# The two-chunk scan of a hybrid trunk, taken as one chunk, with the logs of scan and forgetting summed together

## The chip, the cores and the metric

The kernel runs on one core of one Trainium2 chip, on TensorE (PE), VectorE (DVE), ScalarE (ACT), GpSimd (POOL) and the DMA queues, which SyncE (SP) and ACT feed. The metric is device time in microseconds, the median of several runs; lower is better.

## The reference, cut to what matters

A trunk of two residual layers over 256 tokens of width 1024. Each layer projects the normalised stream by one wide matrix and feeds three causal mixers: a state-space scan (16 heads of 64, 4 groups that share keys `b` and queries `c` of 128 states, chunks of 128 tokens), sliding-window attention, and forgetting attention (16 heads). Their outputs are projected, gated, merged and added to the stream.

```python
def ssd_chunked_scan(xh, dt, a, bm, cm):
    ...
    x_dt = x * dtc[..., None]
    ...
    a_cum = jnp.cumsum(a_dt, axis=-1)
    seg = a_cum[..., :, None] - a_cum[..., None, :]
    decay = jnp.where(causal, jnp.exp(jnp.where(causal, seg, 0.0)), 0.0)
    cb = jnp.einsum('bclgn,bcsgn->bgcls', cc, bc)
    y_diag = jnp.einsum('bgrcls,bcsgrp->bclgrp', cb[:, :, None] * decay, x_dt)
    decay_states = jnp.exp(a_cum[..., -1:] - a_cum)
    states = jnp.einsum('bcsgn,bgrcs,bcsgrp->bcgrpn', bc, decay_states, x_dt)
    ...
    prev = jnp.moveaxis(prev, 0, 1)
    y_off = jnp.einsum('bclgn,bcgrpn,bgrcl->bclgrp', cc, prev, jnp.exp(a_cum))
    return (y_diag + y_off).reshape(b, s, g, r, p)

def forgetting_attention_branch(q, k, v, f_logit, z, f_bias):
    log_f = jax.nn.log_sigmoid((f_logit + f_bias).astype(jnp.float32))
    cum = jnp.transpose(jnp.cumsum(log_f, axis=1), (0, 2, 1))
    ...
        sc = sc + cum[:, :, start:end, None] - cum[:, :, None, :end]
```

Here `a_dt` is `dt` times `a`, the decay logs, summed within a chunk, and `prev` the states, carried from chunk to chunk. With 256 tokens there are two chunks, so one state passes from the first to the second. Of the cumulative logs only differences between two tokens enter the result.

## The kernel before, in words

**Dense work.** Nearly all of the time goes to dense products of the stream with the weights. Each weight tile arrives by a DMA of SP (tile `raw`), is rounded by ACT to a high part (`hi`, L265) and DVE subtracts to get the low part (`lo`, L266); a product then takes three passes (stream high with `hi` and `lo`, stream low with `hi`). There are six buffers each for `raw`, `hi` and `lo`. A dense unit has 24 matmuls, of 256 columns (one block of 128 output channels for all tokens) or of 512 (128 tokens); its sum is held in one of three PSUM buffers `mm`. Five more, `mx`, serve all else.

**Order.** PE runs in an order that the program writes out by hand: the dense units one after the other, and between them, or in the middle of a unit, small pieces of the mixers. A piece is a stretch of a Python generator; it comes due at a time of the program's own clock, which adds a cost for each matmul (L91 to L101), plus a delay that the generator yields (`D_CUM` 12, `D_SSD` 8, `D_SSD2` 3, L25 to L29), and `pump` (L130) puts in what is due. The orders of DVE, ACT and POOL come from a scheduler. Every engine works through its own queue in order; DMAs issued by ACT stand in ACT's queue.

**Decay logs**, once per layer (`decay_logits`, L700 to L753). From a dense product come `dt`, the scan's logs `da` and the forgetting logs `lf`, each two chunks of 128 tokens by 16 heads. `tri` is the matrix of ones up to the diagonal. One pair of products sums `da` with tokens on the partitions (`acum`, L741); a second pair sums it with heads on the partitions (L746); three more do so for `lf`, where the second chunk adds the first through `ones` (L748 to L750). ACT copies both into `cum` and stores them to DRAM (`cumd`, L753), from where they are read back spread over all 128 partitions: for the scan at L785, for forgetting attention as `bias` at L932. The sliding-window attention's pieces (scores on 64-row tiles, softmax, transposes of the weights, second product on 64-wide tiles) follow in PE order, then the scan groups, then forgetting attention.

**A scan group** (`ssd_group`, L780 to L842), four per layer, one at a time, three pieces on PE:

- *Transposes* (L790): four of the inputs, which DVE multiplies by `dt` into `xdt` (L791), and one of the keys, `bt`, copied by ACT (L796). DVE and ACT then make, from the logs spread over the partitions (`bcg`, 128 x 4 heads x 256 tokens): the state's weights `ds` and `xds` (L798 to L801), a decay matrix for each chunk (`decs`, four subtractions with the mask `negtri` at L808, the exponential at L810), and `cx`, the second chunk's queries times the decay since its start (L814, L815).
- *Middle piece*, 8 units of the clock later: the state (`bt` with `xds`, copied by ACT at L821) and for each chunk the product of keys and queries, by which DVE multiplies the decay matrix (L826).
- *Output piece*, 3 units later: for each chunk and each pair of heads the products with `xdt`, and for the second chunk with the state (L838); DVE adds each to the skipped input (L839).

The tiles `bcg` have two buffers (tag L4), `decs` and `cx` share seven (L2).

## Time and profile before

| | |
|---|---|
| median of 3 runs | 844.76 us (847.14, 844.76, 844.22) |
| the profiled execution | 844.62 us |
| its span in the trace | 842.9 us |
| granted PE clock | 0.998 of full speed |
| PE busy | 829.5 us, 98% of the span, 5932 instructions |
| weight loads (PEld) | 758.9 us, 90% |
| DVE, ACT, POOL busy | 641.9, 509.2, 125.8 us |
| DMA | 158.41 MB, 188 GB/s in the mean |

Rows of the trace read: start in us, duration in us, engine, line, operation, output tile <- input tiles, the tile shape on PE (rows*columns), output shape, and "xN" for N instructions recorded as one row from the first start to the last end. A fp32 matmul is recorded as two instructions. The rounded passes of the dense units are one each. Ends of matmuls are modelled, so the distance between starts says more than the duration. A row of a group of instructions gives, behind the count, the busy time in us and the mean of one in ns, then the idle time of the engine just before them and what ended it. Line numbers are those of the kernel before.

### The profile page before, as it was taken

The page shows a single profiled execution, that of the slowest core. Times are in us where ns is not written, and L with a number is a line of the kernel's source. Part 1 is how long each engine was busy: PE and PEld are TensorE (multiplying, and loading weights), DVE is VectorE, ACT ScalarE, POOL GpSimd, SP SyncE. Part 2 cuts the span into 40 slices and gives each one's busy share as a digit, 9 for nine tenths or more (in the row PEclk, how much of TensorE's full clock was granted, in tenths as well). Part 3 has the DMA queues.
Part 4 walks back from the last instruction along what each step waited for, and adds up shares of the span by engine and source line. Part 5 has one row for each costly group of instructions (what it writes and reads, how often), then busy time and mean ns, then how long its engine had stood idle before and what let it go on. Part 6 is the DMA issues. An engine that isn't in the chain of part 4 may idle for free.

```text
span 842.9 us, 15995 instructions
## 1 busy us (share of the span) xinstructions
PE 829.5 (98%) x5932; PEld 758.9 (90%) x5932; DVE 641.9 (76%) x1387; ACT 509.2 (60%) x1012; POOL 125.8 (15%) x166
## 2 busy tenths in 40 slices
PE   7999999999999999999999999999999999999996
PEld 7989898999999998888989998899899999988896
DVE  5778897997776679656688879989878667785665
ACT  6466678665666667435555667775557667654442
POOL 7411300000131010210014112000003110121000
PEclk9999999999999999999999999999999999999999
DMA  8576655676465545648677475565855564566632
GB/s 303 162 231 205 198 171 163 201 210 188 144 201 175 172 164 189 213 151 288 206 233 219 149 204 174 152 212 162 250 176 159 167 179 153 158 237 213 212 101 74
DMA packets 126637, 158.41 MB, mean 188 GB/s; under 512 B 12784, under 2 KB 88224, under 8 KB 126560
## 3 DMA queue, kind: packets, MB, share of 16 engines
q1 hardware_dynamic: 109456, 140.79, 53.2%
q10 hardware_dynamic: 17056, 16.49, 6.3%
q8 instruction: 46, 0.75, 0.4%
q14 instruction: 31, 0.25, 0.1%
q0 software_dynamic: 48, 0.13, 0.0%
HBM read 155.22 MB, written 2.16 MB: 187 GB/s over the span
## 4 chain that ended last, share of the span: by engine, by line
PE 88%; DMA 5%; DVE 2%; issue 2%; ACT 1%; POOL 0%; ACTq 0%; SPq 0%; POOLq 0%; DVEq 0%
PE mm L97 75%; PE mx L97 9%; PE mx L101 3%; DMA raw<-in_w_in_dram 3%; DMA raw<-in_w_proj_dram 1%; DVE lo L266 1%; DMA L<-in_x_dram 1%; DVE L L1068 0%; DVE L L1091 0%; ACT hi L260 0%; ACT hi L265 0%; ACTq L260 0%; POOL sm L227 0%; ACT L L216 0%; DVE L L266 0%
## 5 line engine op out<-in xcount | busy, mean ns | idle before, releaser
L266 DVE TENSOR_TENSOR lo<-raw,hi 128x1024 fp32r<-128x1024 f32 x252 | 307.8, 1234 | 93.4 <-ACT hi L265 84.7
L97 PE MATMUL mm<-hi,L 128*128 128x512 f32 (+1 forms) x1344 | 372.8, 363 | 1.9 <-ACT hi L1225 1.4
L97 PE MATMUL mm<-L,hi 128*128 128x256 f32 x1792 | 317.8, 278 | 0.9 <-DVE L L474 0.9
L265 ACT ACTIVATE hi<-raw 128x1024 fp32r<-128x1024 f32 x252 | 262.9, 1055 | 87.1 <-PE mm L97 59.5
L97 PEld LDWEIGHTS mm<-L,hi 128*128 128x128 f32 x1792 | 277.6, 192 | 7.9 <-issue 3.5
L97 PEld LDWEIGHTS mm<-hi,L 128*128 128x128 f32 x1344 | 241.1, 189 | 32.3 <-issue 2.4
L97 PE MATMUL mm<-L,lo 128*128 128x256 f32 x896 | 246.4, 275 | 0.0
L97 PE MATMUL mm<-lo,L 128*128 128x512 f32 (+1 forms) x672 | 241.3, 360 | 1.4 <-POOL lo L1226 1.4
L97 PEld LDWEIGHTS mm<-L,lo 128*128 128x128 f32 x896 | 171.9, 192 | 0.1
L97 PEld LDWEIGHTS mm<-lo,L 128*128 128x128 f32 x672 | 126.9, 189 | 16.4 <-POOL lo L1226 1.9
L939 POOL TENSOR_SCALAR_AFFINE_SELECT bias<-bias 128x128 f32<-128x128 f32 x64 | 38.6, 635 | 269.4 <-DMA bias<-cumd 237.7
L770 DVE SCALAR_TENSOR_TENSOR L<-L,vec,L 128x255 f32<-128x255 f32 (+2 forms) x96 | 47.5, 495 | 3.6 <-ACT L L767 2.2
L97 PE MATMUL mx<-L,L 128*64 128x128 f32 (+1 forms) x384 | 34.4, 314 | 0.0
L963 ACT ACTIVATE L<-L 128x512 f32<-128x512 f32 x24 | 15.1, 630 | 30.1 <-DVE L L962 30.1
L562 ACT ACTIVATE pp<-pp,nm 128x128 f32<-128x128 f32 x64 | 28.2, 443 | 6.9 <-DVE nm L556 6.9
L97 PEld LDWEIGHTS mx<-L,L 128*64 128x64 f32 x384 | 23.0, 136 | 9.4 <-issue 2.0
L637 ACT ACTIVATE pp<-pp,nm 128x128 f32<-128x128 f32 x64 | 25.1, 393 | 10.3 <-DVE nm L630 9.0
L854 ACT ACTIVATE L<-mm 128x256 f32<-128x256 f32 x48 | 18.2, 379 | 19.5 <-PE mm L97 19.4
L662 POOL TENSOR_SCALAR_AFFINE_SELECT L<-L 128x256 f32<-128x256 f32 x16 | 10.2, 639 | 114.5 <-ACT L L660 114.5
L773 ACT ACTIVATE L<-L 128x256 f32<-128x256 f32 x32 | 13.3, 417 | 21.6 <-DVE L L770 20.4
L630 DVE CUSTOM_DVE_ANT_0 pp<-mx,wmask,nsink 128x128 f32<-128x128 f32 x64 | 24.0, 413 | 2.0 <-PE mx L97 2.0
L1008 POOL TENSOR_TENSOR L<-L,L 128x512 f32<-128x512 f32 x8 | 15.9, 1995 | 57.9 <-DVE L L1007 32.1
(184 smaller groups left out, 795.6 us busy)
## 6 DMA issues: line engine op xcount, KB each, us to landing
raw<-in_w_in_dram SPq DMA_DIRECT2D x200, 512.0 KB, 4.5
raw<-in_w_proj_dram SPq DMA_DIRECT2D x48, 512.0 KB, 5.3
raw<-in_w_out_dram SPq DMA_DIRECT2D x16, 512.0 KB, 5.0
L<-cumd ACTq DMA_DIRECT2D x8, 512.0 KB, 3.9
bias<-cumd ACTq DMA_DIRECT2D x16, 256.0 KB, 3.6
L<-in_gate_bias_dram ACTq DMA_DIRECT2D x12, 256.0 KB, 3.8
L<-in_x_dram SPq DMA_DIRECT2D x2, 512.0 KB, 4.9
nwb<-in_norm_w_dram SPq DMA_DIRECT2D x1, 512.0 KB, 5.3
```

What stands on the lines that cost most here:

```text
L97: nc.tensor.matmul(o, a, b, **kw)
L101: nc.tensor.transpose(o, a, i)
L265: keep(act)(hi, src, AF.Copy)
L266: keep(tt)(lo, src, hi.bitcast(F32), op=ALU.subtract)
L562: act(pp[:, i, sl], pp[:, i, sl], AF.Exp, scale=-1.0, bias=nm[:, e:e + 1], accum_out=sums[:, e:e + 1])
L630: nc.vector.tensor_tensor_reduce(out=pp[:, i, sl], in0=score(p, i, b), in1=m, scale=-0.125, scalar=ns[:, i:i + 1], op0=ALU.add, op1=ALU.mi ...
L637: act(pp[:, i, sl], pp[:, i, sl], AF.Exp, scale=-1.0, bias=nm[:, e:e + 1], accum_out=sums[:, e:e + 1])
L770: stt(a[:, s:S], x_[:, 0:S - s], y.vec[:, 16 * j + u:16 * j + u + 1], a[:, s:S], op0=ALU.mult, op1=ALU.add)
L854: act(halves(th), p, AF.Tanh, scale=0.5)
L939: nc.gpsimd.affine_select(out=bias[:, i, dst], in_=bias[:, i, src], compare_op=ALU.is_ge, fill=NEG, base=0, pattern=[[-1, P]], channel_mul ...
L963: act(g, g, AF.Tanh, scale=0.5)
L1008: gtt(m, m, g, op=ALU.add)
```

## The change

**Logs.** They are measured from the middle of the sequence: the second chunk sums from its start (`tri`), the first backwards from its end (`behind`, which is `tri` less one, so that token t gets minus the sum of the tokens after it). No chunk needs the other's total, and `da` and `lf` (times −16 here, where −8 and 2 were used apart) lie in one tile `dl`, so one pair of products, 32 rows high, gives both. The three products for `lf` go, and one of the two copies.

**Scan.** No state is made. The first chunk's keys meet all 256 queries, and the second chunk's keys the second half. So the decay matrices are `dec` (first chunk's keys, 256 queries), made in place in the tile into which the logs are loaded, and `own` (second chunk's, 128 queries). The transposed keys, `ds`, `xds`, `cx`, the state and their copies and products go. The middle piece has two products into one PSUM tile, 256 and 128 columns wide; the output piece has for each pair of heads one PSUM tile of 256 tokens, with one evacuation.

```diff
@@ in the set-up (pools: "st=2" leaves BUFS)
-    negtri = T("negtri", [P, P])
+    negtri = T("negtri", [P, 2 * P])
...
+    behind = T("behind", [P, P])
+    nc.gpsimd.tensor_scalar(behind, tri, -1.0, None, op0=ALU.add)
+    upto = (behind, tri)
-        lf = T("lf", [P, 2, 16])
+        dl = T("dl", [P, 2, 32])
+        da, lf = dl[:, :, 0:16], dl[:, :, 16:32]
         w = T("uw", [P, 2, 32])
         ts(w[:, :, 0:16], u[:, :, 0:16], 0.0, 0.5, op0=ALU.max, op1=ALU.mult)
         tt(y.dt, w[:, :, 0:16], q3[:, :, 0:16], op=ALU.add)
         ts(y.dt, y.dt, 2.0, None, op0=ALU.mult)
         ts(w[:, :, 16:32], u[:, :, 16:32], 0.0, 0.5, op0=ALU.min, op1=ALU.mult)
         tt(lf, w[:, :, 16:32], q3[:, :, 16:32], op=ALU.subtract)
-        ts(lf, lf, 2.0, None, op0=ALU.mult)
-        da = T("da", [P, 2, 16])
+        ts(lf, lf, -16.0, None, op0=ALU.mult)
         tt(da, y.dt, bc(y.nega, 1, 2), op=ALU.mult)
         yield D_CUM
 
         pa = pmx()
         for c in range(2):
-            mm(pa[:, 16 * c:16 * c + 16], tri, da[:, c, :], start=True, stop=True)
+            mm(pa[:, 16 * c:16 * c + 16], upto[c], da[:, c, :], start=True, stop=True)
         y.acum = T("acum", [P, 2, 16])
         act(y.acum, pa[:, 0:32].rearrange("p (t c) -> p t c", t=2), AF.Copy)
-        cum = T("L2", [16, 2, S])
+        cum = T("L1", [32, S])
         pr = pmx()
         for c in range(2):
-            mm(pr[0:16, c * P:(c + 1) * P], da[:, c, :], tri, start=True, stop=True)
-        act(cum[:, 0, :], pr[0:16, 0:S], AF.Copy)
-        pf = pmx()
-        mm(pf[0:16, 0:P], lf[:, 0, :], tri, start=True, stop=True)
-        mm(pf[0:16, P:S], lf[:, 0, :], ones, start=True, stop=False)
-        mm(pf[0:16, P:S], lf[:, 1, :], tri, start=False, stop=True)
-        act(cum[:, 1, :], pf[0:16, 0:S], AF.Copy, scale=-8.0)
-        y.cumd = dr.tile([16, 2, S], F32, name=f"cumd{y.l}", tag=f"cumd{y.l}")
+            mm(pr[0:32, c * P:(c + 1) * P], dl[:, c, :], upto[c], start=True, stop=True)
+        act(cum, pr[0:32, 0:S], AF.Copy)
+        y.cumd = dr.tile([32, S], F32, name=f"cumd{y.l}", tag=f"cumd{y.l}")
         nc.scalar.dma_start(y.cumd, cum)
 
 
...
         yield lambda: not any(m[2] == 1 for m in waiting)
         yield "ssd"
         xdt = T("L2", [P, 2, 256])
-        bcg = T("L4", [P, 4, S])
-        nc.scalar.dma_start(bcg, y.cumd[4 * g:4 * g + 4, 0, :].partition_broadcast(P))
+        dec = T("L4", [P, 4, S])
+        nc.scalar.dma_start(dec, y.cumd[4 * g:4 * g + 4, :].partition_broadcast(P))
         hs = slice(4 * g, 4 * g + 4)
         for t in range(2):
             p = pmx()
...
                 transpose(p[:, j * P:(j + 1) * P], y.xs[:, 2 * g + j, t * P:(t + 1) * P], ident)
             tt(xdt[:, t, :].rearrange("p (h d) -> p h d", h=4),
                p[:, 0:256].rearrange("p (h d) -> p h d", h=4), bc(y.dt[:, t, hs], 2, 64), op=ALU.mult)
+        own = T("L2", [P, 4, P])
+        for h in range(4):
+            stt(own[:, h, :], dec[:, h, P:S], y.acum[:, 1, 4 * g + h:4 * g + h + 1], negtri[:, 0:P], op0=ALU.subtract, op1=ALU.add)
+        act(own, own, AF.Exp)
+        for h in range(4):
+            stt(dec[:, h, :], dec[:, h, :], y.acum[:, 0, 4 * g + h:4 * g + h + 1], negtri,
+                op0=ALU.subtract, op1=ALU.add)
+        act(dec, dec, AF.Exp)
+        yield D_SSD
+
         p = pmx()
-        transpose(p[:, 0:P], y.bcT[:, g, 0:P], ident)
-        bt = T("bt", [P, P])
-        act(bt, p[:, 0:P], AF.Copy)
-        ds = T("ds", [P, 4], bufs=2)
-        tt(ds, bcg[:, :, P - 1], y.acum[:, 0, hs], op=ALU.subtract)
-        act(ds, ds, AF.Exp)
-        xds = T("L1", [P, 256])
-        tt(xds.rearrange("p (h d) -> p h d", h=4), xdt[:, 0, :].rearrange("p (h d) -> p h d", h=4),
-           bc(ds, 2, 64), op=ALU.mult)
-        decs = []
-        for c in range(2):
-            tk = slice(c * P, (c + 1) * P)
-            dec = T("L2", [P, 4, P])
-            for h in range(4):
-                stt(dec[:, h, :], bcg[:, h, tk], y.acum[:, c, 4 * g + h:4 * g + h + 1], negtri,
-                    op0=ALU.subtract, op1=ALU.add)
-            act(dec, dec, AF.Exp)
-            decs.append(dec)
-
-        cx = T("L2", [P, 4, P])
-        act(cx, bcg[:, :, P:S], AF.Exp)
-        tt(cx, cx, bc(y.bcT[:, 4 + g, P:S], 1, 4), op=ALU.mult)
-        yield D_SSD
-
-        p = pmx()
-        mm(p[:, 0:256], bt, xds, start=True, stop=True)
-        st = T("st", [P, 256])
-        act(st, p[:, 0:256], AF.Copy)
-        for c in range(2):
-            tk = slice(c * P, (c + 1) * P)
-            p = pmx()
-            mm(p[:, 0:P], y.bcT[:, g, tk], y.bcT[:, 4 + g, tk], start=True, stop=True)
-            tt(decs[c], decs[c], bc(p[:, 0:P], 1, 4), op=ALU.mult)
+        mm(p[:, 0:S], y.bcT[:, g, 0:P], y.bcT[:, 4 + g, :], start=True, stop=True)
+        mm(p[:, S:S + P], y.bcT[:, g, P:S], y.bcT[:, 4 + g, P:S], start=True, stop=True)
+        tt(dec, dec, bc(p[:, 0:S], 1, 4), op=ALU.mult)
+        tt(own, own, bc(p[:, S:S + P], 1, 4), op=ALU.mult)
         yield D_SSD2
-        for c in range(2):
-            tk = slice(c * P, (c + 1) * P)
-            for j in range(2):
-                u = 2 * g + j
-                py = pmx()
-                for s in range(c + 1):
-                    for i in range(2):
-                        h = 2 * j + i
-                        hc = slice(64 * h, 64 * h + 64)
-                        a, b = (xdt[:, c, hc], decs[c][:, h, :]) if s == 0 else (st[:, hc], cx[:, h, :])
-                        mm(py[64 * i:64 * i + 64, 0:P], a, b, start=(s == 0), stop=(s == c))
-                stt(y.xs[:, u, tk], y.xs[:, u, tk], y.dsk[:, u:u + 1], py[:, 0:P],
-                    op0=ALU.mult, op1=ALU.add)
+        for j in range(2):
+            u = 2 * g + j
+            py = pmx()
+            for s in range(2):
+                for i in range(2):
+                    h = 2 * j + i
+                    mm(py[64 * i:64 * i + 64, s * P:S], xdt[:, s, 64 * h:64 * h + 64],
+                       (dec, own)[s][:, h, :], start=(s == 0), stop=(s == 1))
+            stt(y.xs[:, u, :], y.xs[:, u, :], y.dsk[:, u:u + 1], py[:, 0:S], op0=ALU.mult, op1=ALU.add)
         yield D_EVAC
         tokens["ssd"] += 1
 
...
         for p in range(2):
             bias = T("bias", [P, 2, 3 * P])
             nc.scalar.dma_start(bias[:, :, P:3 * P],
-                                y.cumd[2 * (j + p):2 * (j + p) + 2, 1, :].partition_broadcast(P))
+                                y.cumd[16 + 2 * (j + p):18 + 2 * (j + p), :].partition_broadcast(P))
             bs.append(bias)
         yield D_BDMA
         for bias in bs:
```

The first place is the piece of the decay logs. PE before, with `mm_1005` and `mm_1050` the dense units around it, `mx_1033` the sums by tokens, `mx_1039` and `mx_1043` the two by heads:

```order
L97 MATMUL mm_1005<-L_24_151,hi_907 128x256
L97 MATMUL mx_1033<-da_838,tri_76 128x16 x2
L97 MATMUL mx_1039<-tri_76,da_838 16x128 x2
L97 MATMUL mx_1043<-tri_76,lf_830 16x128
L97 MATMUL mx_1043<-ones_86,lf_830 16x128
L97 MATMUL mx_1043<-tri_76,lf_830 16x128
L97 MATMUL mm_1050<-L_23_150,hi_889 128x256
L97 MATMUL mm_1050<-L_23_150,lo_890 128x256
L97 MATMUL mm_1050<-L_24_151,hi_889 128x256
```

PE of the changed kernel at the same place (`mx_1034` by tokens, `mx_1040` by heads; `L_51_267` and `qt_454` are keys and queries of the sliding-window attention):

```order
L97 MATMUL mm_1006<-L_25_153,hi_908 128x256
L97 MATMUL mx_1034<-dl_832,behind_98 128x16
L97 MATMUL mx_1034<-dl_832,tri_76 128x16
L97 MATMUL mx_1040<-behind_98,dl_832 32x128
L97 MATMUL mx_1040<-tri_76,dl_832 32x128
L97 MATMUL mx_1050<-L_51_267,qt_454 128x128
L97 MATMUL mx_1051<-L_51_267,qt_454 128x128
L97 MATMUL mx_1050<-L_51_267,qt_454 128x256
L97 MATMUL mx_1051<-L_51_267,qt_454 128x256
```

The three products into `mx_1043` are gone, and the attention's scores, which before came after a further dense unit, follow directly. From there to the end of the first scan groups the mixers' pieces stand about one 256-column unit earlier among the dense units.

The second place is the middle and output pieces of scan group 0 on PE. Before (`mm_2142`, `mm_2210` and `mm_2256` are dense units; the middle piece is `mx_2189` to `mx_2196`):

```order
L97 MATMUL mm_2142<-L_24_151,hi_1971 128x256
L97 MATMUL mx_2189<-L_406_2008,bt_2003 128x256
L97 MATMUL mx_2193<-L_239_1165 128x128
L97 MATMUL mx_2196<-L_239_1165 128x128
L97 MATMUL mm_2210<-hi_2073,L_442_2199 128x512
```

and, one 512-column unit further on:

```order
L97 MATMUL mm_2210<-lo_2174,L_442_2199 128x512
L97 MATMUL mx_2236<-L_407_2010,L_399_1990 64x128 x2
L97 MATMUL mx_2240<-L_407_2010,L_399_1990 64x128 x2
L97 MATMUL mx_2244<-L_408_2016,L_399_1990 64x128 x2
L97 MATMUL mx_2244<-L_409_2022,st_2191 64x128 x2
L97 MATMUL mx_2250<-L_408_2016,L_399_1990 64x128 x2
L97 MATMUL mx_2250<-L_409_2022,st_2191 64x128 x2
L97 MATMUL mm_2256<-hi_2073,L_442_2199 128x512
```

In the changed kernel the middle piece is

```order
L97 MATMUL mm_2090<-L_25_153,hi_1999 128x256
L97 MATMUL mx_2125<-L_239_1171 128x256
L97 MATMUL mx_2125<-L_239_1171 128x128
L97 MATMUL mm_2130<-L_24_152,hi_1987 128x256
L97 MATMUL mm_2130<-L_24_152,lo_1988 128x256
L97 MATMUL mm_2130<-L_25_153,hi_1987 128x256
```

and the output piece

```order
L97 MATMUL mm_2188<-lo_2075,L_432_2177 128x512
L97 MATMUL mx_2201<-L_392_1960,L_391_1959 64x256 x2
L97 MATMUL mx_2201<-L_395_1970,L_391_1959 64x128 x2
L97 MATMUL mx_2207<-L_392_1960,L_391_1959 64x256 x2
L97 MATMUL mx_2207<-L_395_1970,L_391_1959 64x128 x2
L97 MATMUL mm_2188<-hi_2143,L_432_2177 128x512
```

The middle piece has two products in place of three, and the output piece four lines in place of six, now in the middle of a 512-column unit (`mm_2188`) and not behind one. DVE at the same place in the changed kernel, from the splits of the weights (L269 of the changed kernel) to the first multiply by keys and queries (L804); L768 and L772 are the convolution, `mx_2125` the middle piece:

```order
L269 TENSOR_TENSOR lo_2075<-raw_1872,hi_2074 128x1024
L768 SCALAR_TENSOR_TENSOR L_404_2033<-L_405_2034,vec_660,L_404_2033 128x255
L269 TENSOR_TENSOR L_433_2178<-L_153_712,L_432_2177 128x2x256
L768 SCALAR_TENSOR_TENSOR L_404_2033<-L_405_2034,vec_660,L_404_2033 128x254
L269 TENSOR_TENSOR lo_2144<-raw_1935,hi_2143 128x1024
L768 SCALAR_TENSOR_TENSOR L_404_2033<-L_405_2034,vec_660,L_404_2033 128x253
L269 TENSOR_TENSOR lo_2162<-raw_1947,hi_2161 128x1024
L772 SCALAR_TENSOR_TENSOR L_364_1826<-L_406_2040,L_404_2033 128x256
L768 SCALAR_TENSOR_TENSOR L_414_2080<-L_415_2081,vec_660,L_414_2080 128x255
L269 TENSOR_TENSOR L_433_2178<-L_153_712,L_432_2177 128x2x256
L768 SCALAR_TENSOR_TENSOR L_414_2080<-L_415_2081,vec_660,L_414_2080 128x254
L804 TENSOR_TENSOR L_392_1960<-L_392_1960,mx_2125 128x1024
```

The multiply is 1024 columns wide, and stands behind three splits in this piece, with one more and the subtractions of the group ahead of these rows.

The third place is ACT, where the logs of scan group 2 are fetched. Before (with what each waits for; `L_515_2562` is group 2's `bcg`):

```order
L265 ACTIVATE hi_2155<-raw_1939 128x1024 [waits DMAHW4_49,PE_49]
L265 ACTIVATE hi_2173<-raw_1951 128x1024 [waits DMAHW5_49,PE_49]
L785 DMA L_515_2562<-cumd_1048 128x4x256 [waits Activation_49]
L773 ACTIVATE L_413_2057<-L_411_2050 128x256 [waits DVE_49]
L766 ACTIVATE L_422_2098<-mm_2060 128x256
L767 ACTIVATE L_421_2097<-mm_2060,vec_658 128x256
L265 ACTIVATE hi_2263<-raw_1963 128x1024 [waits DMAHW6_49,PE_49]
```

and in the changed kernel (`L_492_2493` is group 2's `dec`):

```order
L764 ACTIVATE L_419_2116<-mm_2090 128x256
L765 ACTIVATE L_418_2115<-mm_2090,vec_660 128x256
L268 ACTIVATE hi_2245<-raw_2003 128x1024 [waits DMAHW7_49,PE_49]
L783 DMA L_492_2493<-cumd_1044 128x1024 [waits PE_49]
L771 ACTIVATE L_420_2122<-L_418_2115 128x256 [waits DVE_49,Activation_49]
L764 ACTIVATE L_430_2168<-mm_2130 128x256
L765 ACTIVATE L_429_2167<-mm_2130,vec_660 128x256
L268 ACTIVATE hi_2279<-raw_2060 128x1024 [waits DMAHW0_49,PE_49]
```

The DMA of the changed kernel waits for PE, whose last reading of group 0's `dec` frees the buffer. Before, its buffer was freed by ACT's own exponential, and DVE's subtractions ahead of that.

More of the change, by code (lines that the diff above doesn't have):

```diff
@@ L59, in hybrid_trunk @@
     BUFS = dict(raw=N_RAW, hi=N_SPLIT, lo=N_SPLIT, L8=8, L4=2, L2=7, L1=14, pp=2, qt=4,
-                bias=2, st=2, sm=6)
+                bias=2, sm=6)
     count = [0]
@@ L170, in hybrid_trunk @@
                             pattern=[[1, P]], channel_multiplier=-1)
-    negtri = T("negtri", [P, P])
+    negtri = T("negtri", [P, 2 * P])
     nc.gpsimd.memset(negtri, 0.0)
-    nc.gpsimd.affine_select(out=negtri, in_=negtri, compare_op=ALU.is_ge, fill=NEG, base=0,
+    nc.gpsimd.affine_select(out=negtri[:, 0:P], in_=negtri[:, 0:P], compare_op=ALU.is_ge, fill=NEG, base=0,
                             pattern=[[1, P]], channel_multiplier=-1)
```

## The prediction

> **What bounds the kernel now.** I read the page's busy shares and its chain first.
>
> ```profile
> PE 829.5 (98%) x5932; PEld 758.9 (90%) x5932; DVE 641.9 (76%) x1387; ACT 509.2 (60%) x1012; POOL 125.8 (15%) x166
> PE 88%; DMA 5%; DVE 2%; issue 2%; ACT 1%; POOL 0%; ACTq 0%; SPq 0%; POOLq 0%; DVEq 0%
> ```
>
> The first row says that TensorE (PE) runs in 98% of the span, the second that 88% of the chain that ended last is PE. That is a mean over stages, so I next asked for the stages in which the changed work lies: the decay logs and attention (75 to 150 us) and the four scan groups of layer 0 (150 to 245) and of layer 1 (562 to 657).
>
> ```profile
> 75.00:150.00 75.00, 75.00 (x547) 66.37 (x545) 64.03 (x156) 56.25 (x132) 11.16 (x20) 1.00 0.59 181
> 150.00:245.00 95.00, 95.00 (x750) 88.12 (x750) 82.33 (x190) 58.95 (x118) 7.80 (x8) 1.00 0.62 188
> 562.00:657.00 95.00, 95.00 (x752) 87.96 (x750) 82.38 (x188) 58.86 (x118) 7.65 (x8) 1.00 0.62 189
> ```
>
> The columns are the stretch, its length, PE, weight loads, DVE, ACT, POOL, the granted clock, and DMA. PE is busy in all of the 95 us, at full clock, while DVE has 95.00 − 82.33 = 12.7 us to spare and ACT 36. A modelled end of a matmul can hide small gaps, so below I go by the distance from one start to the next. Since each piece of the scan stands in one fixed PE order between dense matmuls, a microsecond taken out of PE there is a microsecond of the kernel, as long as nothing that PE needs comes later than PE does.
>
> **The decay logs: three matmuls and a change of shape less, per layer.** The timeline of PE around them:
>
> ```profile
> 73.42 0.52 PE L97 MATMUL mx<-da,tri 128*128 128x16 f32 x4
> 73.87 0.61 PE L97 MATMUL mx<-tri,da 128*16 128x128 f32 x4
> 74.32 0.38 PE L97 MATMUL mx<-tri,lf 128*16 128x128 f32 x2
> 74.54 0.38 PE L97 MATMUL mx<-ones,lf 128*16 128x128 f32 x2
> 74.75 0.38 PE L97 MATMUL mx<-tri,lf 128*16 128x128 f32 x2
> 75.07 0.38 PE L97 MATMUL mm<-L,hi 128*128 128x256 f32 x1
> 77.51 0.28 PE L97 MATMUL mm<-L,hi 128*128 128x256 f32 x1
> 77.62 0.28 PE L97 MATMUL mm<-L,lo 128*128 128x256 f32 x1
> 77.74 0.28 PE L97 MATMUL mm<-L,hi 128*128 128x256 f32 x1
> 77.94 1.58 PE L97 MATMUL mx<-L,qt 64*128 64x128 f32 x16
> ```
>
> Each fp32 product is two records. The three products of the forgetting log start at 74.32, 74.54 and 74.75, so each costs 0.22: they go, 3 × 0.22 = 0.65. The two products above them that remain now write 32 rows and not 16; their 128 columns stay, and by the rows columns set the time, so I cost that at nothing (at worst a row twice as long, +0.45 per layer; at best nothing). The dense matmuls follow each other at 0.11 (77.51, 77.62), but from 77.74 to the 64-row tiles at 77.94 it is 0.20, and from the 16-wide tile at 74.75 to 75.07 it is 0.32 instead of 0.22: a change of tile shape costs 0.1. In the changed order the attention's scores follow the decay products directly, so two such changes become one: 0.1. Per layer 0.65 + 0.1 = 0.75, and 1.5 for two.
>
> The Trainium skill, page "TensorEngine Tiling (Array Packing)", section "Key Properties", says that changing the tiling mode drains TensorE. By that the count of changes matters as well as the count of matmuls, and the rows above price the drain at 0.1; without it the sum would be 1.3 in place of 1.5.
>
> One ACT copy of the logs goes too, and DVE's instructions keep their number there; both engines have time left in this stretch, so this is worth nothing. The write of the logs and the biases keep their bytes.
>
> **A scan group: a transpose and half a product less.** The PE rows of group 0, and two pieces of the same shape as the new ones:
>
> ```profile
> 149.97 0.77 PE L101 MATMUL mx<-ident,L 128*128 128x128 f32 x5
> 161.29 0.60 PE L97 MATMUL mx<-L,bt 128*128 128x256 f32 x2
> 161.72 0.61 PE L97 MATMUL mx<-L 128*128 128x128 f32 x4
> 162.09 0.68 PE L97 MATMUL mm<-hi,L 128*128 128x512 f32 x2
> 167.44 0.88 PE L97 MATMUL mx<-L,L 128*64 128x128 f32 x12
> 168.15 0.39 PE L97 MATMUL mx<-L,st 128*64 128x128 f32 x4
> 168.91 0.70 PE L97 MATMUL mm<-hi,L 128*128 128x512 f32 x2
> 89.24 0.60 PE L101 MATMUL mx<-ident,pp 128*128 128x128 f32 x4
> 82.33 1.52 PE L97 MATMUL mx<-L,L 128*64 128x256 f32 x16
> 83.78 0.38 PE L97 MATMUL mm<-L,hi 128*128 128x256 f32 x1
> ```
>
> Five transposes are recorded at 149.97 and four at 89.24; durations 0.77 and 0.60 differ by 0.17, and inside the four the step is (0.60 − 0.27)/3 = 0.11, with 0.27 the length of one. I take 0.11. The middle piece goes from one 256-wide and two 128-wide products to one 256-wide and one 128-wide: one 128-wide product less, two records of 0.11, so 0.22. The output piece becomes, for each of two head pairs, two 256-wide and two 128-wide products on 64-wide tiles; that is exactly the shape of the sliding window's second product at 82.33, which takes 83.78 − 82.33 = 1.45 where the old one takes 168.91 − 167.44 = 1.47. Saved: 0.01 or so. Per group 0.11 + 0.22 + 0.01 = 0.34, for eight groups 2.7.
>
> Against the profiled execution of 844.62: 844.62 − 1.5 − 2.7 = 840.4. It lies 0.14 under the median of 844.76, so no correction is due.
>
> **What the other engines do, and why it costs little.** Prices of the groups' DVE and ACT work:
>
> ```profile
> L808 DVE SCALAR_TENSOR_TENSOR L<-L,acum,negtri 128x128 f32<-128x128 f32 x64 | 17.5, 345 | 0.0
> L826 DVE TENSOR_TENSOR L<-L,mx 128x512 f32<-128x512 f32 x16 | 10.4, 681 | 0.0
> L839 DVE SCALAR_TENSOR_TENSOR L<-L,dsk,mx 128x128 f32<-128x128 f32 x32 | 9.3, 341 | 0.0
> L895 DVE SCALAR_TENSOR_TENSOR L<-L,vec,mx 128x256 f32<-128x256 f32 x16 | 6.9, 474 | 0.0
> L815 DVE TENSOR_TENSOR L<-L,L 128x512 f32<-128x512 f32 x8 | 5.5, 685 | 0.0
> L801 DVE TENSOR_TENSOR L<-L,ds 128x256 f32<-128x256 f32 x8 | 3.3, 415 | 0.0
> 163.90 0.68 DVE L826 TENSOR_TENSOR L<-L,mx 128x512 f32<-128x512 f32 x1
> 164.52 0.43 DVE L774 SCALAR_TENSOR_TENSOR L<-L,L 128x256 f32<-128x256 f32 x1
> 164.86 0.68 DVE L826 TENSOR_TENSOR L<-L,mx 128x512 f32<-128x512 f32 x1
> 157.77 2.35 DVE L266 TENSOR_TENSOR lo<-raw,hi 128x1024 fp32r<-128x1024 f32 x2
> ```
>
> DVE drops L815 and L801 (0.69 + 0.42 us) and trades four evacuations of 0.34 for two of about 0.47, the price of L895; four of the eight L808 become 256 wide, +0.13 each by the same pair of rows; the first multiply goes from 512 to 1024 columns, and as the next instruction starts 0.62 after one of 512 (163.90 to 164.52), to 0.68 + 0.6 = 1.28. About 0.6 of DVE is saved per group, and three ACT passes. Both are off the path and worth nothing here.
>
> What can cost is lateness. The output products at 167.44 wait for both multiplies; the second ends at 164.86 + 0.68 = 165.54, 1.9 us ahead, and that is the cover now. In the changed PE order all pieces from the scores on stand one 256-wide dense unit earlier, but the dense work between a group's transposes, middle piece and output stays nearly what it was, so the cover carries over as far as DVE keeps its pace. In the changed DVE order the subtractions, four splits, five taps of the convolution two half splits, a gate's multiply and a convolution's end stand between the transposed inputs and the multiply, about 11.5 us in all: 2.6 + 4 × 1.2 + 5 × 0.4 + 2 × 0.6 + 0.6 + 0.35; with the transposed inputs and the two multiplies, the second ends about 14.3 us after the transposes, and PE wants it about 17.1 us after them (167.44 − 149.97 = 17.5 less the 0.33 saved ahead). So the cover is 2.8 by that sum, and 1.9 − 0.6 − 0.33 = 0.97 if the old order's cover is taken, less the wider multiply and the PE time saved ahead of it. Either way I take no wait, and set 0.2 us for small ones over the whole kernel.
>
> The decay tile now is the tile that the logs land in, and PE's last output product reads it. So the log transfers of groups 2 and 3 wait for that product, and they are issued by ACT, which stands behind them:
>
> ```profile
> L<-cumd ACTq DMA_DIRECT2D x8, 512.0 KB, 3.9
> 156.14 0.37 ACTq L785 DMA_DIRECT2D L<-cumd  x1
> 160.15 1.06 ACT L265 ACTIVATE hi<-raw 128x1024 fp32r<-128x1024 f32 x1 [1.12 <-PE mm L97]
> 164.39 0.37 ACT L766 ACTIVATE L<-mm 128x256 f32<-128x256 f32 x1
> ```
>
> Group 2's transfer went out at 156.14. Now it goes out after 168, lands 3.9 later, and group 2 is worked on only after group 1, about a quarter of the 95 us further on: no cost in the landing. ACT however reaches it about 13.5 us after the transposes (163.5) and stands some 4 us. Behind it are an evacuation of the next dense unit, whose accumulator is taken again only three units later, and a weight split that PE reads only after one and a half 512-wide and two 256-wide units, over 10 us later. The same row at 160.15 shows that ACT's splits wait for PE to free a buffer anyway. So this hides, at up to 4 us; if the cover were gone it would be 4 us in group 0 of both layers, 8 in all.
>
> The start gains one POOL instruction on 128x128 for the table `behind`. Bounds: nothing, as POOL is 15% busy, and 0.6 us if its 128x128 pass stood on the path; I take nothing, since the tables are used tens of microseconds later.
>
> **The rivals.** *The saved time is given back.* PE comes 0.3 us earlier to weights or operands that are no earlier, and waits there. For it: in 150 to 245 us DVE is at 87%, the next engine to bind. Against it: PE shows no gap at the pieces, and the row at 160.15 has ACT waiting for PE, not PE for ACT. At full effect 844.6; with half of the gain lost 842.5.
>
> *Slower: the multiply comes late.* All eight groups' outputs wait for DVE's wide multiply, because one more pair of splits stands ahead of it than I count. A pair is 2.35 us (157.77), and the least cover 0.97, so PE waits 1.38 per group: 8 × 1.38 = 11, giving 840.4 + 11 = 851.4, and with two pairs ahead 870. The kernel is slower than before from 4.2/8 = 0.5 us of wait per group, so when the multiply is 0.97 + 0.5 = 1.5 us later than that cover has it. Against it: DVE has 12.7 us in 95 to catch up, and its work falls.
>
> *Weight loads bind.*
>
> ```profile
> L97 PEld LDWEIGHTS mx<-L,L 128*64 128x64 f32 x384 | 23.0, 136 | 9.4 <-issue 2.0
> ```
>
> The removed products also remove about 12 loads per group and 6 per layer in the logs. Of 136 to 190 ns each, 8 × 12 × 0.16 + 12 × 0.14 = 17 us would go if loads ran one after the other: 827.6. Against it: at 167.44 twelve products of that kind start within 0.71 us, where 12 × 0.136 = 1.6 us of loads would not fit, so loads of half-width tiles overlap each other.
>
> The Trainium skill, page "Perfetto Trace Analysis", section "Identifying the Most-Contended Engine", says to judge TensorE by the busy share of its weight loads, not of its matmuls, since those are pipelined. It would make this rival the forecast; the twelve products in 0.71 us speak against it.
>
> **How the numbers follow.** Forecast: 0.66, its own range 839.4 to 841.8 (the unknown 0.45 per layer of the wider rows, and 0.2 to 1.2 of small waits). Given back: 0.18, 841.8 to 845. Late multiply: 0.12, mostly around 851 and beyond. Loads: 0.04, 828. The likeliest is 840.4 + 0.2 = 840.6. The range 839.0 to 846.0 holds the first two, 0.84. A measurement of this kernel can tell about 0.5% from no change, 844.76 ± 4.2: the lower line, 840.54, runs through the middle of the forecast. So faster is half of 0.66 and 0.04, 0.37; slower is what of the late multiply lies over 849, 0.10; the rest, 0.53, is the same.
>
> **What would show it.** In the changed profile: four transposes and not five per group, a middle piece of 0.58, an output piece of 1.45; the decay piece 0.65 shorter and followed by the scores; PE still 95 of 95 in the groups' stretch. A wait of PE on the wide multiply, or idle time of PE on splits behind a standing ACT, would show the rivals. The prediction is wrong if the sum of PE's starts falls as said and the span doesn't.

## The result, and the profile after

The changed kernel takes 840.31 us (median of 4 runs, 840.03 to 840.80) against 845.16 us of the kernel before in the same comparison (844.22 to 847.14): a ratio of 0.994, with a 95% interval of 0.9926 to 0.9954. The forecast was 840.6. Its profiled execution took 840.80 us with a span of 839.1, 3.8 us under the 842.9 of before. Line numbers of the changed kernel differ from those of before by up to 25: L266 became L269, L785 L783, L826 L804 and L805, L839 L815, L1012 L987.

The page of the changed kernel, its busy shares and its chain:

```profile
PE 824.1 (98%) x5832; PEld 752.4 (90%) x5832; DVE 642.5 (77%) x1347; ACT 502.9 (60%) x978; POOL 130.3 (16%) x167
PE 91%; DMA 5%; DVE 1%; issue 1%; ACT 1%; POOL 0%; SPq 0%; POOLq 0%; DVEq 0%; ACTq 0%
```

PE has 100 instructions and 5.4 us less, and the chain is still PE's. The two stretches of the scan groups, with the columns as in the prediction:

```profile
150.00:245.00 95.00, 95.00 (x721) 86.77 (x721) 82.61 (x169) 56.88 (x105) 7.75 (x8) 1.00 0.64 195
562.00:657.00 95.00, 95.00 (x722) 86.76 (x721) 82.09 (x168) 56.98 (x105) 8.66 (x12) 1.00 0.62 193
```

PE is still busy in 95 of 95 us where the groups lie. The pieces on PE: the logs, then of group 0 the transposes, the middle piece and the output piece, each with the dense matmul behind it:

```profile
73.28 0.29 PE L97 MATMUL mx<-dl,behind 128*128 128x16 f32 x2
73.42 0.37 PE L97 MATMUL mx<-dl,tri 128*128 128x16 f32 x2
73.73 0.41 PE L97 MATMUL mx<-behind,dl 128*32 128x128 f32 x2
73.97 0.38 PE L97 MATMUL mx<-tri,dl 128*32 128x128 f32 x2
74.28 1.58 PE L97 MATMUL mx<-L,qt 64*128 64x128 f32 x16
75.79 0.38 PE L97 MATMUL mm<-L,hi 128*128 128x256 f32 x1
...
146.39 0.66 PE L101 MATMUL mx<-ident,L 128*128 128x128 f32 x4
146.80 0.68 PE L97 MATMUL mm<-hi,L 128*128 128x512 f32 x2
157.51 0.82 PE L97 MATMUL mx<-L 128*128 128x256 f32 x4
158.09 0.36 PE L97 MATMUL mm<-L,hi 128*128 128x256 f32 x1
163.53 1.52 PE L97 MATMUL mx<-L,L 128*64 128x256 f32 x16
164.99 0.48 PE L97 MATMUL mm<-hi,L 128*128 128x512 f32 x1
```

From start to start the logs take 1.00 us (73.28 to 74.28), where they took 1.64 (73.42 to 75.07), and 32 rows cost 0.01 more than 16 did. The middle piece takes 0.58 and not 0.80, the output piece 1.45.

Because the order of PE is fixed, the same dense matmul can be found in both traces, and the distance between two of them compares the kernels whatever came earlier. I take the stretch from the first product of the logs to the first dense matmul behind the forgetting scores that follow group 3's output. These two pieces end it, before and then after:

```profile
237.77 0.88 PE L97 MATMUL mx<-L,L 128*64 128x128 f32 x12
238.47 0.39 PE L97 MATMUL mx<-L,st 128*64 128x128 f32 x4
...
239.23 1.89 PE L97 MATMUL mx<-qt 64*128 64x128 f32 x16
241.05 0.38 PE L97 MATMUL mm<-L,hi 128*128 128x256 f32 x1
```

```profile
235.42 1.52 PE L97 MATMUL mx<-L,L 128*64 128x256 f32 x16
236.87 1.58 PE L97 MATMUL mx<-qt 64*128 64x128 f32 x16
238.38 0.38 PE L97 MATMUL mm<-L,hi 128*128 128x256 f32 x1
```

The stretch was 241.05 − 73.42 = 167.62 (from unrounded starts) and is 238.38 − 73.28 = 165.10: 2.52 us less, and in layer 1 to the hundredth the same. So PE lost 5.04 us of work, not the 4.2 forecast. The forgetting scores (`mx<-qt`) are not touched by the change, and yet they take 1.51 us (236.87 to 238.38) where they took 1.82.

The span fell by less than 5.04. The largest loss is near the end of layer 0, at 385 us, where PE waits for the merged branches, which it transposes for the output projection. The experiments call this place the layer boundary. Before, PE and ACT there:

```profile
386.10 0.66 PE L101 MATMUL mx<-ident,L 128*128 128x128 f32 x4 [0.70 <-DVE L L1012]
378.01 1.06 ACT L265 ACTIVATE hi<-raw 128x1024 fp32r<-128x1024 f32 x1 [5.77 <-DMA raw<-in_w_in_dram]
```

and after:

```profile
384.81 0.66 PE L101 MATMUL mx<-ident,L 128*128 128x128 f32 x4 [2.07 <-DVE L L987]
376.73 1.06 ACT L268 ACTIVATE hi<-raw 128x1024 fp32r<-128x1024 f32 x1 [6.51 <-DMA raw<-in_w_in_dram]
```

In brackets stands how long an engine waited, and for what. PE names DVE, but DVE waited for a weight tile's high part, and ACT, which makes it, for that tile's DMA. PE came 2.7 us earlier, the DMA only 1.3, so 1.37 is lost. The sum of the profiled executions: −5.04, +1.37 here, +0.15 in the first 18 us, −0.28 at the scores of the sliding-window attention at 52 us, which makes −3.8, the difference of the spans.

### The profile page after: what moved, and what is told of

Same layout as the page of the kernel before. It is cut to its first block, busy times and chain, and to the rows that moved or that the text cites. A ratio compares the mean times of both kernels' runs of the same rounds, so it can differ in the third digit from the quotient of the medians.

```text
span 839.1 us, 15714 instructions
## 1 busy us (share of the span) xinstructions
PE 824.1 (98%) x5832; PEld 752.4 (90%) x5832; DVE 642.5 (77%) x1347; ACT 502.9 (60%) x978; POOL 130.3 (16%) x167
## 4 chain that ended last, share of the span: by engine, by line
PE 91%; DMA 5%; DVE 1%; issue 1%; ACT 1%; POOL 0%; SPq 0%; POOLq 0%; DVEq 0%; ACTq 0%
PE mm L97 79%; PE mx L97 9%; PE mx L101 4%; DMA raw<-in_w_in_dram 3%; DMA raw<-in_w_proj_dram 2%; DVE lo L269 0%; DMA hb<-in_sinks_dram 0%; ACT hi L268 0%; POOL lo L1201 0%; ACT hi L1200 0%; DVE L L474 0%; ACT L L1060 0%; DVE L L269 0%; DVE L L987 0%; DVE L L986 0%
## 5 line engine op out<-in xcount | busy, mean ns | idle before, releaser
L269 DVE TENSOR_TENSOR lo<-raw,hi 128x1024 fp32r<-128x1024 f32 x252 | 307.8, 1236 | 88.1 <-ACT hi L268 80.8
L768 DVE SCALAR_TENSOR_TENSOR L<-L,vec,L 128x255 f32<-128x255 f32 (+2 forms) x96 | 46.8, 488 | 6.5 <-ACT L L765 5.1
L97 PE MATMUL mx<-L,L 128*64 128x128 f32 (+1 forms) x384 | 36.5, 332 | 0.0
L665 POOL TENSOR_SCALAR_AFFINE_SELECT L<-L 128x256 f32<-128x256 f32 x16 | 11.9, 743 | 109.2 <-ACT L L663 109.2
L101 PE MATMUL mx<-ident,L 128*128 128x128 f32 x144 | 22.3, 279 | 3.7 <-DVE L L987 2.1
```

What stands on the lines that cost most here:

```text
L97: nc.tensor.matmul(o, a, b, **kw)
L101: nc.tensor.transpose(o, a, i)
L269: keep(tt)(lo, src, hi.bitcast(F32), op=ALU.subtract)
L768: stt(a[:, s:S], x_[:, 0:S - s], y.vec[:, 16 * j + u:16 * j + u + 1], a[:, s:S], op0=ALU.mult, op1=ALU.add)
```

## The experiments

"Stretch" in the table is the distance just defined, in layer 0 (layer 1 agrees within 0.02 but for e7, 168.99). "Boundary" is the distance between two dense matmuls 8 apart around 385 us, with the transposes between them.

| kernel | ratio to before (95%) | stretch | boundary |
|---|---|---|---|
| before | 1 | 167.62 | 3.00 |
| changed | 0.994 (0.9926 to 0.9954) | 165.10 | 4.37 |
| e1, logs alone | 0.9987 (0.9969 to 1.0005) | 166.79 | 3.22 |
| e2, scan alone | 0.9963 (0.9949 to 0.9977) | 165.94 | 4.22 |
| e3, changed, four output tiles | 0.994 (0.9921 to 0.996) | 165.45 | 3.58 |
| e4, before, two output tiles | 0.9997 (0.9981 to 1.0014) | 167.32 | 2.94 |
| e5, changed, skip weights by rows | 0.9902 (0.9883 to 0.9921) | 165.10 | 2.08 |
| e6, before, skip weights by rows | 0.998 (0.9968 to 0.9993) | 167.62 | 2.08 |
| e7, changed, multiply late | 1.0029 (1.0016 to 1.0043) | 169.17 | 4.79 |
| e8, e5 with the old places | 0.9905 (0.9886 to 0.9925) | 165.30 | 2.08 |

**e1: the logs alone.** The changed kernel with the scan of before; the state has one buffer.

```diff
+        bcg = T("L4", [P, 4, S])
+        nc.scalar.dma_start(bcg, y.cumd[4 * g:4 * g + 4, :].partition_broadcast(P))
...
+        mm(p[:, 0:256], bt, xds, start=True, stop=True)
+        st = T("st", [P, 256])
```

> The logs' part alone: logs from the middle of the sequence, one pair of products for both, while the scan still makes its state (one buffer for the state instead of two, for space). Theory of separate PE terms: the piece of the logs with the scores behind it is 0.73 to 0.75 us shorter in each layer and nothing else of PE changes, so the span falls by 1.5 us, less what the first layer's part (0.75) loses at the layer boundary, where PE waits for weights that land by another clock: 0.8 to 1.5 us under before, so a ratio near 0.9985. The scores of forgetting attention behind group 3's output still take 1.82 us (as before) by the theory of too few PSUM buffers. Rival, that the gain comes from the pieces standing one dense unit earlier and not from the work removed: as the order here is that of the changed kernel, most of its 4.85 us would be here, a ratio of 0.995.

Median 843.75 against 845.19. The stretch is 0.83 shorter in each layer, 1.66 in both: this is the logs' part. The scores behind group 3 still take 1.82. The order is that of the changed kernel, so the pieces' places are not the gain.

**e2: the scan alone.** The changed kernel with the logs of before, apart from the `behind` for the first chunk.

```diff
-            mm(pr[0:32, c * P:(c + 1) * P], dl[:, c, :], upto[c], start=True, stop=True)
+            mm(pr[0:16, c * P:(c + 1) * P], da[:, c, :], upto[c], start=True, stop=True)
+        mm(pf[0:16, 0:P], lf[:, 0, :], tri, start=True, stop=True)
+        mm(pf[0:16, P:S], lf[:, 0, :], ones, start=True, stop=False)
+        mm(pf[0:16, P:S], lf[:, 1, :], tri, start=False, stop=True)
```

> The scan's part alone: no state, as in the changed kernel, while the forgetting logs still have three products of their own. Theory of separate PE terms: 0.34 us per group, 2.75 in all, and 0.31 us per layer behind the last group's output, 0.62, together 3.4; of the first layer's half (1.7) up to 0.9 is lost at the layer boundary, so 2.5 to 3.4 us under before, a ratio of 0.996 to 0.997. The pieces stand where they stood before. Rival, that the position of the pieces makes the gain: about 1 us or less under before.

Median 842.09. The stretch is 1.68 shorter per layer: 4 × 0.34 = 1.37, and 0.31 behind group 3. With e1's 0.83 that is 2.51 of the 2.52: the two parts add up, and nothing is left over.

**e3: the changed kernel with four output tiles.** Each of 128 tokens, as before, the products otherwise the new ones.

```diff
-        for j in range(2):
-            u = 2 * g + j
-            py = pmx()
+        for c in range(2):
+            for j in range(2):
+                u = 2 * g + j
+                py = pmx()
...
+                stt(y.xs[:, u, tk], y.xs[:, u, tk], y.dsk[:, u:u + 1], py[:, 0:P], op0=ALU.mult, op1=ALU.add)
```

> The changed kernel, but the output piece writes four PSUM tiles of 128 tokens again and evacuates each, with the same decay matrices and no state. Theory that the forgetting scores behind group 3's output wait for PSUM buffers: four output tiles and four score tiles share five buffers, so the scores take 1.82 us again in place of 1.51, +0.31 us per layer; the output pieces cost +0.01 each. Together +0.6 to +0.7 us over the changed kernel. Rival, that the scores ran faster for another reason (the pieces' place, or the missing state): the scores stay at 1.51 and the time within 0.1 us of the changed kernel's.

The timeline of e3 at group 3:

```profile
235.90 1.53 PE L97 MATMUL mx<-L,L 128*64 128x128 f32 x24
237.36 1.89 PE L97 MATMUL mx<-qt 64*128 64x128 f32 x16
239.19 0.38 PE L97 MATMUL mm<-L,hi 128*128 128x256 f32 x1
```

The scores take 1.82 again, and the stretch is 0.35 longer. The median (840.37 against 840.31) does not show the 0.6 to 0.7 expected: the boundary was 0.8 shorter than the changed kernel's in the profiles. So this rests on the trace.

**e4: the kernel before with two output tiles.** The reverse, with no product changed.

```diff
-        for c in range(2):
-            for j in range(2):
-                py = pmx()
+        for j in range(2):
+            py = pmx()
+            for c in range(2):
...
```

> The kernel before, with only the output piece's PSUM tiles changed: two of 256 tokens instead of four of 128, evacuated in two instructions; all products as before. Theory of the PSUM buffers: the scores behind group 3's output go from 1.82 to 1.51 us in both layers, 0.62 us of PE less; as half of it is in the first layer and may be lost at the boundary, 0.3 to 0.6 us under before. Rival: the scores stay at 1.82 and nothing moves.

```profile
239.28 0.39 PE L97 MATMUL mx<-L,st 128*64 128x128 f32 x4
239.60 1.58 PE L97 MATMUL mx<-qt 64*128 64x128 f32 x16
241.11 0.38 PE L97 MATMUL mm<-L,hi 128*128 128x256 f32 x1
```

The scores take 1.51, the stretch is 0.31 shorter in both layers. The median is 844.41 against 845.19, and the interval of the ratio holds 1, so this too rests on the trace. Why: four output tiles and the four of the scores share five PSUM buffers, and the buffers come free when DVE evacuates. Before, DVE began that only as the scores began (239.23):

```profile
239.15 1.11 DVE L839 SCALAR_TENSOR_TENSOR L<-L,dsk,mx 128x128 f32<-128x128 f32 x4
```

The single records of the trace show where the 0.31 goes. The scores run on 64-row tiles, two side by side, into one PSUM tile each. In the changed kernel and in e4 the first products of the two start within 0.01 us. Before, the first starts at 239.23 and the other at 239.54, just after the first evacuation has ended (239.49). The half of PE that began late ends 0.31 later. As the other half works meanwhile, the profile counts PE as busy.

**e5 and e6: the skip weights by rows.** In both kernels the skip weights of a layer come by two strided DMAs of 4-byte elements; here they come as one row spread over the partitions, and DVE picks them apart.

```diff
-        for i, v in enumerate((dt_bias, f_bias, sinks, a_log)):
...
+        for i, v in enumerate((dt_bias, f_bias, sinks, a_log, d_skip)):
             pdma(y.hb[:, 16 * i:16 * i + 16], v[l:l + 1, :].to_broadcast([P, 16]))
...
-        for half in range(2):
-            src = d_skip[l:l + 1, :].rearrange("o (j two) -> two o j", two=2)[half]
-            pdma(y.dsk[64 * half:64 * half + 64, :], src.to_broadcast([64, NK]))
...
+            pin(ts)(y.dsk[rows, :], y.hb[rows, 64:80].rearrange("p (j two) -> p two j", two=2)[:, half, :],
+                    1.0, None, op0=ALU.mult)
```

> The changed kernel, with the skip weights of each layer loaded as a sixteen-wide row spread over the partitions, like the other constants, and picked apart by two small DVE instructions, in place of two strided loads of 4-byte elements. Theory that these two strided loads hold up the weight load issued behind them (issued at 363.84 us and landed at 376.62 in the changed kernel, while the DMA engines stood idle): the weight load lands within 6 us of its issue, ACT's wait of 6.5 us for it goes, and PE's wait of 2.1 us at 385 us falls to about 0, so 1.5 to 2.2 us under the changed kernel. Rival, that the weight load is late because of its place in the SP queue or its buffers: the wait at 385 stays at 2 us and the time does not move by over 0.5 us.

> The kernel before with the same edit to the loads of the skip weights. Theory that the strided loads set PE's wait at the layer boundary: PE's wait of 0.7 us at 386 us goes, so 0.5 to 0.9 us under before; and the difference between the changed kernel and before, both with this edit, is then all of the PE time removed, 5.3 us in place of 3.9 in the span. Rival: the boundary does not move, and the two kernels stay 3.9 us apart.

The DMAs from 353 to 378 us, ahead of the boundary. The first row is the busy share of the 16 DMA engines in 40 slices of 0.625 us, in tenths. The others are issues, with the median time to landing at the end. The changed kernel:

```profile
DMA  7444889889787400000000000000123589999999
...
raw<-in_w_in_dram SPq DMA_DIRECT2D x4, 512.0 KB, 8.6
raw<-in_w_proj_dram SPq DMA_DIRECT2D x4, 512.0 KB, 11.1
...
dsk<-in_d_skip_dram ACTq DMA_DIRECT2D x2, 2.0 KB, 8.1
```

and e5, with the ACT instruction that had waited 6.5 us for a DMA:

```profile
DMA  0167999999830009498889997798989997467996
...
raw<-in_w_in_dram SPq DMA_DIRECT2D x4, 512.0 KB, 4.5
raw<-in_w_proj_dram SPq DMA_DIRECT2D x4, 512.0 KB, 7.8
...
hb<-in_d_skip_dram ACTq DMA_DIRECT2D x1, 8.0 KB, 3.7
```

```profile
371.98 1.06 ACT L268 ACTIVATE hi<-raw 128x1024 fp32r<-128x1024 f32 x1 [3.89 <-PE mm L97]
```

The 8.6 lies midway between the two landings that the trace has: the load issued at 354.73, ahead of the strided ones, took 4.5 us, and the one issued at 363.84, behind them, 12.8. In e5 the load issued at 363.44 took 4.5. In the changed kernel the DMA engines stood idle from 361.75 to 370.5 us, most of it with that load under way, in e5 for 1.9 us. So in that time it was not the traffic of other transfers that kept the load waiting. At which step the strided loads hold it back is not shown.

ACT now waits for PE, and the boundary is 2.08 in both kernels: 2.29 shorter in the changed one, 0.92 in the one before. A stall at the window scores at 52 us goes too (0.9 us in the changed kernel), there behind layer 0's strided loads. The expectations did not count it, and both gains are larger than expected. e5 has a median of 837.52 us (837.50 to 837.80), 2.8 under the changed kernel: the best version here. e6 has 843.56, 1.7 under before. The two are 6.0 apart, more than the 5.04, and the fastest runs 5.0 (842.49 and 837.50). In e6's profile PE waits at the start of layer 1, where neither the changed kernel nor e5 does:

```profile
424.72 0.48 PE L97 MATMUL mm<-hi,L 128*128 128x512 f32 x1 [1.05 <-DVE sm L220]
```

e1 has the same wait. Both have the old scan, but so have the kernel before and e4, whose traces do not show the wait, so the old scan alone does not bring it. What does stays open.

**e7: the multiply late.** Two more passes of DVE over the wide decay matrix.

```diff
         tt(dec, dec, bc(p[:, 0:S], 1, 4), op=ALU.mult)
+        for _ in range(2):
+            stt(dec, dec, 1.0, dec, op0=ALU.mult, op1=ALU.max)
```

> The changed kernel with two more passes over the wide decay matrix on DVE behind its multiply in each group (each writes the same values again), about 1.2 us each, so that the output's operands come 2.3 us later. In the changed kernel the second multiply ends 1.7 us (group 0), 2.0 (group 1), 3.4 (group 2) ahead of the output piece. Theory that this cover hides lateness until it is used up: PE waits 0.6 and 0.3 us in groups 0 and 1 and nothing in group 2, 1 to 3 us in both layers together, plus what DVE's added 2.4 us per group costs the weight splits (9.6 us of the 12.4 us that DVE has free in the groups' 95 us): up to 4 us more. Rival, that the multiply is already what PE waits for: 2.3 us in each of eight groups, 18 us over the changed kernel.

The waits of PE in e7 (what waited, for what: us in total, times, longest):

```profile
PE mx L97 <- DVE L L806: 6.0, 6, 1.3
PE mx L101 <- DVE L L989: 2.5, 1, 2.5
PE mx L97 <- DVE L L807: 0.7, 2, 0.3
```

L806 is the added pass. The median is 848.00, 7.7 over the changed kernel, and in the trace the two stretches are 4.07 and 3.89 longer. PE's waits for L806 and L807 make 6.7 of that: more than the 1 to 3 expected for the waits, far under the rival's 18. PE waits in three groups of four. The scheduler puts convolution taps of 0.4 us between the passes, so in group 0 the operands come 3.4 us later rather than 2.3. The cover is there, and it is short.

**e8: the old places.** e5 with the planner's clock charged for the three removed products.

```diff
             mm(pr[0:32, c * P:(c + 1) * P], dl[:, c, :], upto[c], start=True, stop=True)
+        clock["t"] += 0.654
```

> The changed kernel with the skip weights loaded as rows (as in e5), and with the program's clock charged 0.654 us behind the products of the logs, what the three removed products had cost it. No instruction changes, but all pieces stand where the kernel before had them: the scores come one dense unit behind the logs, not directly. Theory that joining two pieces of different tile shape saves one change of shape, which costs 0.09 us on the way in and 0.10 on the first dense matmul behind: the logs' part then saves 0.65 us per layer and not 0.84, so PE's time from the logs to the end of the groups is 0.19 us longer per layer than in e5, 0.4 in all: 837.9 us. Rival, that the pieces' new places matter by themselves (other waits, other PSUM turns): a difference from e5 of 1 us or more, either way.

```profile
73.10 0.38 PE L97 MATMUL mm<-L,hi 128*128 128x256 f32 x1
73.31 0.28 PE L97 MATMUL mm<-L,lo 128*128 128x256 f32 x1
...
75.66 0.28 PE L97 MATMUL mm<-L,lo 128*128 128x256 f32 x1
75.77 0.28 PE L97 MATMUL mm<-L,hi 128*128 128x256 f32 x1
75.97 1.58 PE L97 MATMUL mx<-L,qt 64*128 64x128 f32 x16
```

Median 838.04, 0.5 over e5; the stretch is 0.20 longer in both layers. Behind the logs the first dense matmul takes 0.21 (73.10 to 73.31) where others take 0.11, and ahead of the scores the last takes 0.20 (75.77 to 75.97). So a change of tile shape costs 0.1 on the last matmul ahead of it and 0.1 on the first behind it, and joining the pieces saves one change, 0.2. Behind a piece that keeps the shape the first dense matmul takes 0.19 too (158.09 to 158.28 behind the changed kernel's middle piece), but there the piece's own last step is 0.08 shorter than usual, and nothing is lost.

## Why the prediction was right, point by point

The mechanism was the one forecast: PE's work in a fixed order sets the time, and less of it makes the kernel faster. That the median came within 0.3 us is partly luck, as two errors of opposite sign nearly cancel: in the profiled executions PE's work fell by 0.84 us more than forecast, and waits took back 1.0 more. The medians fell by 4.85, with an interval of 3.9 to 6.3 by the ratio's, too wide to show that loss.

- *The logs, 1.5.* Measured 1.66. The three products were right (0.65), and 32 rows cost 0.01 more than 16. The change of shape was mis-sized: 0.1 was counted for the matmul ahead of it alone, and the first one behind pays 0.1 as well (e8). What the Trainium skill says in "TensorEngine Tiling (Array Packing)", section "Key Properties", that a change of mode drains TensorE, agrees with both rows; the number is this case's.
- *The groups, 2.7.* Measured 8 × 0.34 = 2.75 (e2). The transposes (0.41 in place of 0.52 from start to start), the middle piece and the output piece came out as priced.
- *What the sum lacked.* 0.31 us per layer behind the last group. The prediction counted DVE's four evacuations against two and called them off the path. They were, except where they free PSUM buffers for the next piece: there half as many tiles let the scores run without a break (e3, e4).
- *Small waits, 0.2.* The profiled execution lost 1.2. This is the rival of time given back, in part: PE came earlier to operands that were not as much earlier. But it was not where the rival looked for it. PE didn't wait for splits in the groups' stretch, which stayed at 95 of 95, but at the layer boundary, for a weight tile held up behind two strided loads (e5, e6).
- *The multiply late.* It did not happen, and the forecast's covers (2.8 by the order, 0.97 by the old one) lie around the measured one:

```profile
159.67 1.22 DVE L804 TENSOR_TENSOR L<-L,mx 128x1024 f32<-128x1024 f32 x1
160.80 0.48 DVE L768 SCALAR_TENSOR_TENSOR L<-L,vec,L 128x253 f32<-128x253 f32 x1
161.19 0.68 DVE L805 TENSOR_TENSOR L<-L,mx 128x512 f32<-128x512 f32 x1
```

  The second multiply ends at 161.87, 15.5 us after the transposes where 14.3 was forecast, and 1.66 us ahead of the output piece at 163.53. The wide one takes 1.22, where 1.28 was counted. e7 shows the other side: once the cover is spent, the kernel is slower than before (848.00 against 845.29).
- *ACT behind the transfer of group 2's logs.* It stood, and it was hidden:

```profile
162.41 1.05 ACT L268 ACTIVATE hi<-raw 128x1024 fp32r<-128x1024 f32 x1
164.88 0.34 ACTq L783 DMA_DIRECT2D L<-cumd  x1
165.87 0.42 ACT L771 ACTIVATE L<-L 128x256 f32<-128x256 f32 x1 [2.40 <-DVE L L768]
```

  From 163.46 to 164.88 ACT waits for PE's last reading: 1.4 us and not 4, since ACT got there 17.1 us after the transposes (146.39) and not 13.5. No wait of PE follows in the groups.
- *Weight loads.* 100 loads went (108 were counted), 6.5 us of their busy time, and the time fell by 4.85, not 17. e4 removes no load and still saves 0.31 per layer; the starts of the products account for all 5.04. The Trainium skill, in "Perfetto Trace Analysis", section "Identifying the Most-Contended Engine", judges how close TensorE is to its limit by the busy share of its weight loads, next to its rate of operations. That share is 90% in both profiles, and it does not say what an edit saves: the 17 came from adding up loads that overlap, and the traces don't bear it out.

## What to carry to other kernels

Where PE's order is fixed and PE never idles, price an edit by the distance from start to start in that order, count both sides of a change of tile shape (0.1 us each here), and then ask which buffers the edit frees and who takes them next. Compare two traces between the same two dense matmuls: here that gave 2.52 in both layers to the hundredth, while the median of the kernel before moved by 0.7 us from one comparison to the next (844.76 to 845.46). A gain ahead of a wait for a transfer is paid out only if the transfer comes earlier too; look for small strided loads ahead of it.

## What the runs showed of the hardware

Two DMAs of 2 KB each, made of 4-byte elements and issued by ACT at 360 us, delayed a 512 KB weight load that SP issued behind them in another queue: it landed after 12.8 us, and in about 6.7 of them the 16 DMA engines stood idle. Without the two, a load at that place took 4.5 us. Without them a stall of 0.9 to 2.3 us goes at either place, behind layer 0's pair and behind layer 1's.

Forgetting scores whose four PSUM tiles were not all free took 1.82 us, and 1.51 when they were. One half of PE started 0.31 us late while the other worked, so no idle time was shown for PE: a busy share of 100% did not show the wait, only the distance between starts.

A change of tile shape on PE cost 0.1 us on the last matmul ahead of it and 0.1 on the first behind it.
